# Strassen products of a feed-forward continued in their PSUM banks, with the mixed weights' sums on GpSimd

## The chip, the cores and the metric

The kernel runs on one core of one Trainium2 chip. The metric is the device time of one execution in microseconds (us). Each time is the median of several runs. The profile is of one more execution, taken by the hardware profiler; its times are counted from the start of its span.

The engines are TensorE (PE; its weight loads are PEld), VectorE (DVE), ScalarE (ACT), GpSimd (POOL) and SyncE (SP), which here only issues DMA transfers. Each works through its own instructions in order and waits on semaphores for the others. PSUM is the memory that TensorE writes its products to; it has eight banks here, seven of which the matrix products rotate through.

## The reference

One step of a hybrid decoder layer over 1032 token columns (1024 of a prompt, 8 single tokens), in float32. Cut to what matters here:

```python
h = rms_norm(x, norm_mix_pre)
q, k, v, u, gates = split(h @ w_in)
a = dilated_attention(q, k, v) @ w_attn_out          # three head groups
c = conformer_conv(u) @ w_conv_out
mix = (sigmoid(gate_a) * a + sigmoid(gate_c) * c) @ w_out
x = x + rms_norm(mix, norm_mix_post)
h2 = rms_norm(x, norm_ffn_pre)
gg, uu = split(h2 @ w_ffn_in)                        # 1024 -> 2 x 2816
f = (silu(gg) * uu) @ w_ffn_out                      # 2816 -> 1024
x = x + rms_norm(f, norm_ffn_post)
x = x + sigmoid(rms_norm(x, ple_norm) @ w_ple_gate) * (p @ w_ple_proj)
```

The change lies in `h2 @ w_ffn_in` and the `silu(gg) * uu` behind it.

## The kernel before, in words

Activations stand transposed: 128 channels on the partitions, the 1032 tokens along the free axis. Each float32 operand is split in two parts, hi (ScalarE rounds it to the format fp32r) and lo (the rest, a subtraction), and a product is three matmuls: hi x hi, hi x lo, lo x hi (`mm3`, L278 to L280). In the profile, names that end in h and l are these parts.

The stages, by the span's clock: attention, convolution and the input projections to about 770 us; w_out, the normalisation chains and the first three of the 22 hidden blocks (`hidden_plain`, j = 0 to 2) to 934; the other 19 hidden blocks (`hidden_strassen`, j = 3 to 21) to 1317; the product with w_ffn_out in five groups to 1560 (`ffn_out`, hidden rows loaded back by `load_hidden`); the embedding stage to the end.

A hidden block j is 128 rows of gg and 128 of uu. `hidden_strassen` computes a 2 x 2 block product (gg and uu by the upper and lower half of the input channels, over two quarters of the tokens) with seven products in place of eight. p = 0, 1 are the two pairs of token quarters (258 columns each); the seven products go in the order 1, 2, 6, 5, 7, 3, 4. Each product is four k steps of three matmuls of 128 x 258, in a bank of its own, and when it ends VectorE or ScalarE reads the bank. The running sums are kept in the four quarters of a tile `pk`: x, v, s, w. VectorE makes one addition out of PSUM for each product after the first, and a second one for product 7. In the end x holds silu(gg) * uu of one quarter and v of the other; a DMA stores them to DRAM (`d_h`).

The weights of the seven products come from `prepare(j)`: from the two loaded weight tiles a and b (`raw`, 128 x 1024 each, halves a1, a2, b1, b2) it makes s1 = b1 + b2, s2 = s1 - a1, s3 = a1 - b1, s4 = a2 - s2, and splits a, the four sums and b2 into hi parts (ScalarE) and lo parts (VectorE): wah/wal for the products 1 and 2, wbh/wbl for 6 and 5, wch/wcl for 7 and 3, wd for 4. `prepare(j + 1)` is a generator, of which one step is taken behind each product of block j; in the last block `first_hidden` takes its place and loads the first four hidden pairs of the next stage. `fetch` and `ensure` load weights three tiles ahead (`rawp`, 3 buffers), so that the load of a tile waits until the one three before it was read.

Nothing sets the order by hand in this part: a scheduler orders each engine's instructions by its own estimate, with the limits that the pools give (43 `act` slots, 4 `sc` and 6 `rl` tiles, the PSUM banks). SP's queue is in order as well: a load that waits for its buffer holds all that stands behind it.

Names that matter below: r is the reciprocal root of a normalisation, on GpSimd (`token_rstd`: a power over 128 x 3); TensorE spreads it over the columns (L337, m<-ident,r). hr is a hidden pair loaded from `d_h`, uh and ul its hi and lo parts (ScalarE, VectorE). L120 is the helper that records every instruction but the matmuls.

Of the kernel before, what the change touches and what calls it, by code (L numbers as in the profile page):

```python
# [16 lines left out]
P = 128  # L17
# [41 lines left out]
def decoder_step(ctx: ExitStack, tc: tile.TileContext, ins, outs):  # L59
# [24 lines left out]
    def act(s, dt=F32):  # L84
        return actp.tile([P, SLOT], dt, tag="act", name=nm(s))
# [9 lines left out]
    def bank():  # L95
        gtags.rotate(-1)
        t = gtags[-1]
        return (psg if t == "g" else psa).tile([P, 512], F32, tag=t, name=nm("g"))
# [166 lines left out]
    def finish(key):  # L265

        while any(ch[2] == key for ch in chains):
            tick(5)
# [5 lines left out]

        return c if isinstance(c, tuple) else CH[c]

    def mm3(ps, n, hi_w, lo_w, xh, xl, first, last):
        TE.matmul(ps, hi_w, xh, start=first, stop=False)  # L278
        TE.matmul(ps, hi_w, xl, start=False, stop=False)  # L279
        TE.matmul(ps, lo_w, xh, start=False, stop=last)  # L280

    def gemm_bank(wi, xs, c, nk=KT, mid=None, at=MID):

# [1041 lines left out]
    def prepare(j):  # L1325
# [6 lines left out]

        def split(src, hi, lo):
            A.activation(hi, src, AF.Copy)
            V.tensor_sub(lo, src, hi.bitcast(F32))

        def halves(hi, lo):
            return [(hi[:, i * H:(i + 1) * H], lo[:, i * H:(i + 1) * H]) for i in range(2)]
# [3 lines left out]
        w[1], w[2] = halves(hi, lo)  # L1342
        yield
        s1, s2 = sc("s1"), sc("s2")
        V.tensor_add(s1, b1, b2)
        V.tensor_sub(s2, s1, a1)
        w[6], w[5] = halves(act("wbh", F32R), act("wbl", F32R))
        split(s2, *w[6])
        yield
        split(s1, *w[5])  # L1350
        yield
        s3 = sc("s3")
        V.tensor_sub(s3, a1, b1)
        w[7], w[3] = halves(act("wch", F32R), act("wcl", F32R))
        split(s3, *w[7])
        yield
        s4 = sc("s4")
        V.tensor_sub(s4, a2, s2)
        split(s4, *w[3])
        yield  # L1360
        d = act("wd", F32R)
        w[4] = d[:, :H], d[:, H:2 * H]
        split(b2, *w[4])

    def hidden_strassen(j, nxt):
        for p in range(2):
            finish(2)
            finish(("t", p))
            t0 = 2 * p * QN
            quarter = {1: (0, 0), 2: (4, 0), 3: (4, QN)}  # L1370
            pk = act("pk")
            x, v, s, w = (pk[:, i * QN:(i + 1) * QN] for i in range(4))
            for m in (1, 2, 6, 5, 7, 3, 4):
                ps = bank()[:, :QN]
                wh, wl = prods[j][m]
                for k in range(4):
                    if m in quarter:
                        f, o = quarter[m]
                        xh, xl = (y[:, t0 + o:t0 + o + QN] for y in h2[f + k])
                    else:  # L1380
                        xh, xl = (y[:, k * QN:(k + 1) * QN] for y in tsum[p][{5: 0, 6: 1, 7: 2, 4: 3}[m]])
                    mm3(ps, QN, wh[:, k * P:(k + 1) * P], wl[:, k * P:(k + 1) * P], xh, xl, k == 0, k == 3)
                if m == 1:
                    A.activation(x, ps, AF.Copy)
                elif m == 2:
                    V.tensor_add(s, x, ps)
                    A.activation(s, s, AF.Silu)
                elif m == 6:
                    V.tensor_add(x, x, ps)
                elif m == 5:  # L1390
                    V.tensor_add(v, x, ps)
                elif m == 7:
                    V.tensor_add(w, v, ps)
                    V.tensor_add(x, x, ps)
                elif m == 3:
                    V.tensor_add(v, v, ps)
                    A.activation(v, v, AF.Silu)
                    V.tensor_mul(v, v, w)
                else:
                    V.tensor_add(x, x, ps)  # L1400
                    V.tensor_mul(x, x, s)
                tick(1.3)
                next(nxt, None)
            SY.dma_start(d_h[j, :, t0:t0 + 2 * QN], pk[:, :2 * QN])
        del prods[j]

    for js, qs in [(range(2), range(2)), ((2,), (0,)), (range(2), (2,)), ((2,), (1, 2))]:
# [250 lines left out]
```

## Time and profile before

| | us |
|---|---|
| median of 3 runs | 1694.67 (1694.48 to 1694.79) |
| span of the profiled execution | 1692.8 |
| TensorE busy | 1676.1 |
| VectorE busy | 1195.4 |
| ScalarE busy | 610.5 |
| GpSimd busy | 23.1 |
| Strassen blocks, 934 to 1318: TensorE busy | 384.00 of 384.00 |
| the same stretch: VectorE, ScalarE busy | 256.29, 119.29 |

The page lists the busy time of each engine and follows the chain of work that ended last. A row of a listing in order of time gives the start and the duration in us, the engine, the line, the operation, output<-inputs, shapes and count, and in brackets the engine's idle time before it with what ended it. A row of a grouped listing gives the count, then the busy us of the group, the mean ns of one, and the idle time ahead of it.

### The profile page before, as it was taken

The page shows a single profiled execution, that of the slowest core. Times are in us where ns is not written, and L with a number is a line of the kernel's source. Part 1 is how long each engine was busy: PE and PEld are TensorE (multiplying, and loading weights), DVE is VectorE, ACT ScalarE, POOL GpSimd, SP SyncE. Part 2 cuts the span into 40 slices and gives each one's busy share as a digit, 9 for nine tenths or more (in the row PEclk, how much of TensorE's full clock was granted, in tenths as well). Part 3 has the DMA queues.
Part 4 walks back from the last instruction along what each step waited for, and adds up shares of the span by engine and source line. Part 5 has one row for each costly group of instructions (what it writes and reads, how often), then busy time and mean ns, then how long its engine had stood idle before and what let it go on. Part 6 is the DMA issues. An engine that isn't in the chain of part 4 may idle for free.

```text
span 1692.8 us, 28641 instructions
## 1 busy us (share of the span) xinstructions
PE 1676.1 (99%) x11651; PEld 1649.1 (97%) x11651; DVE 1195.4 (71%) x2084; ACT 610.5 (36%) x1231; POOL 23.1 (1%) x33
## 2 busy tenths in 40 slices
PE   8999999999999999999999999999999999999998
PEld 7999999999999999999999999999999999999998
DVE  7899879858979686553679666666666445548863
ACT  6434445445343344123445323323323311213520
POOL 1000000000000000000000000000000000000000
PEclk9999999999999999999999999999999999999999
DMA  5241121121354264423242222323333533420411
GB/s 191 65 125 66 44 68 45 61 81 53 102 177 159 92 196 128 142 73 121 85 128 78 82 98 89 100 89 113 111 108 125 182 109 114 162 97 13 159 51 47
DMA packets 80889, 174.64 MB, mean 103 GB/s; under 512 B 11154, under 2 KB 49890, under 8 KB 80374
## 3 DMA queue, kind: packets, MB, share of 16 engines
q1 hardware_dynamic: 80566, 172.69, 31.3%
q8 instruction: 91, 1.49, 0.4%
q0 software_dynamic: 192, 0.13, 0.1%
q14 instruction: 40, 0.33, 0.1%
HBM read 136.16 MB, written 50.13 MB: 110 GB/s over the span
## 4 chain that ended last, share of the span: by engine, by line
PE 92%; DVE 4%; issue 1%; DMA 1%; ACT 1%; POOL 0%; SPq 0%; POOLq 0%; DVEq 0%; ACTq 0%
PE g L278 29%; PE g L280 29%; PE g L279 29%; DVE y L120 3%; PE O L675 1%; PE S L630 1%; PE PT L657 1%; DVE wl L120 1%; PE m L337 0%; DMA res<-d_x 0%; PE m L325 0%; DMA strow<-in_state_conv_dram 0%; DVE acc L120 0%; POOL r L120 0%; DMA raw<-in_w_in_dram 0%
## 5 line engine op out<-in xcount | busy, mean ns | idle before, releaser
L278 PE MATMUL g<-hh,wh 128*128 128x384 f32 (+1 forms) x1200 | 393.1, 328 | 7.1 <-ACT wh L120 7.1
L280 PE MATMUL g<-hh,wl 128*128 128x384 f32 (+1 forms) x1200 | 384.3, 320 | 0.2 <-DVE wl L120 0.2
L279 PE MATMUL g<-hl,wh 128*128 128x384 f32 (+1 forms) x1200 | 383.9, 320 | 0.0
L120 DVE SCALAR_TENSOR_TENSOR y<-z,taps,y 128x1023 f32<-128x1023 f32 (+14 forms) x240 | 303.9, 1267 | 36.7 <-ACT y L120 31.1
L278 PEld LDWEIGHTS g<-hh,wh 128*128 128x128 f32 x1200 | 226.4, 189 | 14.4 <-ACT wh L120 7.1
L279 PEld LDWEIGHTS g<-hl,wh 128*128 128x128 f32 x1200 | 226.3, 189 | 0.6 <-DVE hl L120 0.3
L280 PEld LDWEIGHTS g<-hh,wl 128*128 128x128 f32 x1200 | 225.9, 188 | 0.8 <-DVE wl L120 0.8
L280 PE MATMUL g<-uh,wl 128*128 128x344 f32 x528 | 168.7, 320 | 0.0
L279 PE MATMUL g<-ul,wh 128*128 128x344 f32 x528 | 168.6, 320 | 0.0
L278 PE MATMUL g<-uh,wh 128*128 128x344 f32 x528 | 163.2, 321 | 0.6 <-DVE fa L120 0.6
L120 DVE TENSOR_TENSOR wl<-raw,wh 128x1024 fp32r<-128x1024 f32 x106 | 129.0, 1220 | 35.1 <-ACT wh L120 28.6
L120 DVE TENSOR_TENSOR pk<-pk,g 128x258 f32<-128x258 f32 x266 | 105.4, 420 | 55.1 <-PE g L280 39.3
L120 ACT ACTIVATE wh<-raw 128x1024 fp32r<-128x1024 f32 x106 | 110.7, 1051 | 7.1 <-PE g L279 3.8
L278 PE MATMUL g<-mh,wh 128*128 128x344 f32 x336 | 107.4, 323 | 0.0
L280 PE MATMUL g<-mh,wl 128*128 128x344 f32 x336 | 107.1, 320 | 0.0
L279 PE MATMUL g<-ml,wh 128*128 128x344 f32 x336 | 107.0, 320 | 0.0
L120 DVE TENSOR_TENSOR fa<-fa,g 128x344 f32<-128x344 f32 x96 | 47.1, 510 | 77.2 <-PE g L280 76.7
L279 PEld LDWEIGHTS g<-ul,wh 128*128 128x128 f32 x528 | 99.3, 188 | 0.0
L280 PEld LDWEIGHTS g<-uh,wl 128*128 128x128 f32 x528 | 99.2, 188 | 0.0
L278 PEld LDWEIGHTS g<-uh,wh 128*128 128x128 f32 x528 | 98.0, 188 | 0.9 <-DVE fa L120 0.9
L278 PE MATMUL g<-th,wbh 128*128 128x258 f32 x304 | 86.0, 283 | 0.0
L279 PE MATMUL g<-ml,wah 128*128 128x258 f32 x304 | 85.9, 283 | 0.0
(234 smaller groups left out, 3687.1 us busy)
## 6 DMA issues: line engine op xcount, KB each, us to landing
raw<-in_w_in_dram SPq DMA_DIRECT2D x50, 512.0 KB
raw<-in_w_ffn_in_dram SPq DMA_DIRECT2D x44, 512.0 KB
hr<-d_h SPq DMA_DIRECT2D x22, 516.0 KB
raw<-in_w_ffn_out_dram SPq DMA_DIRECT2D x22, 512.0 KB
d_h<-pk SPq DMA_DIRECT2D x38, 258.0 KB
out_kvs_dram<-in_cache_kv_w_dram SPq DMA_DIRECT2D x16, 510.0 KB
d_x<-mo SPq DMA_DIRECT2D x24, 172.0 KB
out_yT_dram<-fa SPq DMA_DIRECT2D x24, 172.0 KB
```

What stands on the lines that cost most here:

```text
L120: ins = fn(*a, **k)
L278: TE.matmul(ps, hi_w, xh, start=first, stop=False)
L279: TE.matmul(ps, hi_w, xl, start=False, stop=False)
L280: TE.matmul(ps, lo_w, xh, start=False, stop=last)
L630: TE.matmul(sp[h][:, o:o + nk], qT[h * 64:(h + 1) * 64, blk * P:(blk + 1) * P], kT[h * 64:(h + 1) * 64, (blk + 1) * P - nk:(blk + 1) * P], ...
L657: TE.transpose(ps[:, o:o + P], e[:, o:o + P], ident)
L675: TE.matmul(ps[h * 64:(h + 1) * 64, i * P:(i + 1) * P], vtok[:, k0:k0 + 64], self.p[half][:, o:o + P], start=kb == kbs[0], stop=kb == kbs[-1])
```

## The change

It has three parts.

- In `hidden_strassen` (now with a class `Quad`) the products share three banks: 1, 6, 7 and 4 one after the other in B1, 2 in B2, 5 and 3 in B3. Only the products 1, 2 and 5 open a bank; the others add to what is there (`more` in `mm3` marks a group of matmuls that goes on). So a bank holds p1, then p1 + p6, and so on, and the sums that the addition trees made are already there. What is needed of a bank before it is added to is read out first: ScalarE copies it after the products 1, 6 and 5 into `rl` tiles (p1, p6, p5). VectorE adds PSUM to such a copy after 2, 7 and 3, and multiplies PSUM by x after 4.
- For j over 3 the two pairs go product by product (1 of pair 0, 1 of pair 1, 2 of pair 0, ...), with one store of `pk` for each pair at the block's end. Block 3 does one pair after the other.
- In `prepare` the four sums and the six lo parts are made by GpSimd: per block nine operations of 128 x 512 and one of 128 x 1024.

```diff
--- before.py
+++ after.py
@@ -274,10 +274,10 @@
 
         return c if isinstance(c, tuple) else CH[c]
 
-    def mm3(ps, n, hi_w, lo_w, xh, xl, first, last):
-        TE.matmul(ps, hi_w, xh, start=first, stop=False)
-        TE.matmul(ps, hi_w, xl, start=False, stop=False)
-        TE.matmul(ps, lo_w, xh, start=False, stop=last)
+    def mm3(ps, n, hi_w, lo_w, xh, xl, first, last, more=False):
+        TE.matmul(ps, hi_w, xh, start=first, stop=False, skip_group_check=more)
+        TE.matmul(ps, hi_w, xl, start=False, stop=False, skip_group_check=more)
+        TE.matmul(ps, lo_w, xh, start=False, stop=last, skip_group_check=more)
 
     def gemm_bank(wi, xs, c, nk=KT, mid=None, at=MID):
 
@@ -1332,7 +1332,7 @@
 
         def split(src, hi, lo):
             A.activation(hi, src, AF.Copy)
-            V.tensor_sub(lo, src, hi.bitcast(F32))
+            G.tensor_sub(lo, src, hi.bitcast(F32))
 
         def halves(hi, lo):
             return [(hi[:, i * H:(i + 1) * H], lo[:, i * H:(i + 1) * H]) for i in range(2)]
@@ -1342,66 +1342,102 @@
         w[1], w[2] = halves(hi, lo)
         yield
         s1, s2 = sc("s1"), sc("s2")
-        V.tensor_add(s1, b1, b2)
-        V.tensor_sub(s2, s1, a1)
+        G.tensor_add(s1, b1, b2)
+        G.tensor_sub(s2, s1, a1)
         w[6], w[5] = halves(act("wbh", F32R), act("wbl", F32R))
         split(s2, *w[6])
         yield
         split(s1, *w[5])
         yield
         s3 = sc("s3")
-        V.tensor_sub(s3, a1, b1)
+        G.tensor_sub(s3, a1, b1)
         w[7], w[3] = halves(act("wch", F32R), act("wcl", F32R))
         split(s3, *w[7])
         yield
         s4 = sc("s4")
-        V.tensor_sub(s4, a2, s2)
+        G.tensor_sub(s4, a2, s2)
         split(s4, *w[3])
         yield
         d = act("wd", F32R)
         w[4] = d[:, :H], d[:, H:2 * H]
         split(b2, *w[4])
 
+    ORDER = (1, 2, 6, 5, 7, 3, 4)
+    B1, B2, B3 = range(3)
+    BANK = {1: B1, 6: B1, 7: B1, 4: B1, 2: B2, 5: B3, 3: B3}
+    OPENS = (1, 2, 5)
+
+    class Quad:
+
+
+        def __init__(self, j, p):
+            self.j, self.p, self.t0 = j, p, 2 * p * QN
+            self.banks, self.part = {}, {}
+            self.pk = act("pk")
+
+        def piece(self, i):
+            return self.pk[:, i * QN:(i + 1) * QN]
+
+        def operand(self, m, k):
+            quarter = {1: (0, 0), 2: (4, 0), 3: (4, QN)}
+            if m in quarter:
+                f, o = quarter[m]
+                return tuple(y[:, self.t0 + o:self.t0 + o + QN] for y in h2[f + k])
+            return tuple(y[:, k * QN:(k + 1) * QN] for y in tsum[self.p][{5: 0, 6: 1, 7: 2, 4: 3}[m]])
+
+        def product(self, m):
+            if m in OPENS:
+                self.banks[BANK[m]] = bank()[:, :QN]
+            ps = self.banks[BANK[m]]
+            wh, wl = prods[self.j][m]
+            for k in range(4):
+                xh, xl = self.operand(m, k)
+                mm3(ps, QN, wh[:, k * P:(k + 1) * P], wl[:, k * P:(k + 1) * P], xh, xl,
+                    k == 0 and m in OPENS, k == 3, m not in OPENS)
+
+        def after(self, m):
+            x, v = self.piece(0), self.piece(1)
+            ps = self.banks[BANK[m]]
+
+            def keep(name):
+                t = rl(name)[:, :QN]
+                A.activation(t, ps, AF.Copy)
+                self.part[m] = t
+
+            if m == 1:
+                keep("p1")
+            elif m == 2:
+                V.tensor_add(x, self.part[1], ps)
+                A.activation(x, x, AF.Silu)
+            elif m == 6:
+                keep("p6")
+            elif m == 5:
+                keep("p5")
+            elif m == 7:
+                w = self.part[5]
+                V.tensor_add(w, w, ps)
+            elif m == 3:
+                V.tensor_add(v, self.part[6], ps)
+                A.activation(v, v, AF.Silu)
+                V.tensor_mul(v, v, self.part[5])
+            else:
+                V.tensor_mul(x, ps, x)
+
     def hidden_strassen(j, nxt):
-        for p in range(2):
-            finish(2)
-            finish(("t", p))
-            t0 = 2 * p * QN
-            quarter = {1: (0, 0), 2: (4, 0), 3: (4, QN)}
-            pk = act("pk")
-            x, v, s, w = (pk[:, i * QN:(i + 1) * QN] for i in range(4))
-            for m in (1, 2, 6, 5, 7, 3, 4):
-                ps = bank()[:, :QN]
-                wh, wl = prods[j][m]
-                for k in range(4):
-                    if m in quarter:
-                        f, o = quarter[m]
-                        xh, xl = (y[:, t0 + o:t0 + o + QN] for y in h2[f + k])
-                    else:
-                        xh, xl = (y[:, k * QN:(k + 1) * QN] for y in tsum[p][{5: 0, 6: 1, 7: 2, 4: 3}[m]])
-                    mm3(ps, QN, wh[:, k * P:(k + 1) * P], wl[:, k * P:(k + 1) * P], xh, xl, k == 0, k == 3)
-                if m == 1:
-                    A.activation(x, ps, AF.Copy)
-                elif m == 2:
-                    V.tensor_add(s, x, ps)
-                    A.activation(s, s, AF.Silu)
-                elif m == 6:
-                    V.tensor_add(x, x, ps)
-                elif m == 5:
-                    V.tensor_add(v, x, ps)
-                elif m == 7:
-                    V.tensor_add(w, v, ps)
-                    V.tensor_add(x, x, ps)
-                elif m == 3:
-                    V.tensor_add(v, v, ps)
-                    A.activation(v, v, AF.Silu)
-                    V.tensor_mul(v, v, w)
-                else:
-                    V.tensor_add(x, x, ps)
-                    V.tensor_mul(x, x, s)
-                tick(1.3)
-                next(nxt, None)
-            SY.dma_start(d_h[j, :, t0:t0 + 2 * QN], pk[:, :2 * QN])
+        for group in ((0,), (1,)) if j == CLASSIC else ((0, 1),):
+            quads = []
+            for p in group:
+                finish(2)
+                finish(("t", p))
+                quads.append(Quad(j, p))
+            for m in ORDER:
+                for q in quads:
+                    q.product(m)
+                    q.after(m)
+                    tick(1.3)
+                    next(nxt, None)
+            for q in quads:
+                SY.dma_start(d_h[j, :, q.t0:q.t0 + 2 * QN], q.pk[:, :2 * QN])
         del prods[j]
 
     for js, qs in [(range(2), range(2)), ((2,), (0,)), (range(2), (2,)), ((2,), (1, 2))]:
```

How the instructions stand then. GpSimd's queue has 36 rows before and 226 with the change. Around the last normalisation ahead of block 3 it read, before (r1 is a power for one third of the tokens):

```order
L120 TENSOR_TENSOR r1_1129_8420<-r0_1128_8418,mhalf_101 128x3
L120 TENSOR_TENSOR r1_1161_8644<-r0_1160_8642,mhalf_101 128x3
L120 TENSOR_TENSOR r1_1171_8763<-r0_1170_8761,mhalf_101 128x3
L120 TENSOR_TENSOR r1_1210_8996<-r0_1209_8994,mhalf_101 128x3
L120 TENSOR_TENSOR r1_2073_15861<-r0_2072_15859,mhalf_101 128x3
L120 TENSOR_TENSOR r1_2109_16103<-r0_2108_16101,mhalf_101 128x3
```

and it reads with the change:

```order
L120 TENSOR_TENSOR r1_1161_8644<-r0_1160_8642,mhalf_101 128x3
L120 TENSOR_TENSOR r1_1171_8763<-r0_1170_8761,mhalf_101 128x3
L120 TENSOR_TENSOR s1_1269_9429<-raw_1218_9023 128x512
L120 TENSOR_TENSOR s2_1270_9430<-s1_1269_9429,raw_1215_9017 128x512
L120 TENSOR_TENSOR r1_1210_8996<-r0_1209_8994,mhalf_101 128x3
L120 TENSOR_TENSOR s3_1273_9439<-raw_1215_9017,raw_1218_9023 128x512
L120 TENSOR_TENSOR s4_1276_9445<-raw_1215_9017,s2_1270_9430 128x512
L120 TENSOR_TENSOR wal_1268_9426<-raw_1215_9017,wah_1267_9425 128x1024
L120 TENSOR_TENSOR wbl_1272_9434<-s2_1270_9430,wbh_1271_9433 128x512
L120 TENSOR_TENSOR wbl_1272_9434<-s1_1269_9429,wbh_1271_9433 128x512
```

The power r1_1210 now stands behind the sums s1 and s2 of block 3, which wait for the weight tiles raw_1218 and raw_1215.

SyncE's queue at the end of the last block and the start of the next stage, before (pk_1800 and pk_1823 are the two pairs of block 21, hr_1808 to hr_1833 the first four hidden pairs):

```order
L120 DMA hr_1808_13872<-d_h_84 128x1032
L120 DMA raw_1812_13893<-in_w_ffn_out_dram 128x1024
L120 DMA d_h_84<-pk_1800_13808 128x516
L120 DMA hr_1816_13915<-d_h_84 128x1032
L120 DMA raw_1820_13936<-in_w_ffn_out_dram 128x1024
L120 DMA hr_1825_13958<-d_h_84 128x1032
L120 DMA raw_1829_13979<-in_w_ffn_out_dram 128x1024
L120 DMA hr_1833_13999<-d_h_84 128x1032
L120 DMA d_h_84<-pk_1823_13943 128x516
L120 DMA out_kvs2_dram<-in_cache_kv_w2048_dram 16x8160
L120 DMA raw_1846_14112<-in_w_ffn_out_dram 128x1024
L120 DMA hr_1849_14118<-d_h_84 128x1032
```

and with the change (pk_1764 and pk_1765 are the pairs of block 21, hr_1775, hr_1783, hr_1793 and hr_1799 the first four hidden pairs):

```order
L120 DMA hr_1775_13768<-d_h_84 128x1032
L120 DMA raw_1779_13788<-in_w_ffn_out_dram 128x1024
L120 DMA hr_1783_13808<-d_h_84 128x1032
L120 DMA raw_1788_13829<-in_w_ffn_out_dram 128x1024
L120 DMA d_h_84<-pk_1764_13700 128x516
L120 DMA d_h_84<-pk_1765_13701 128x516
L120 DMA out_kvs2_dram<-in_cache_kv_w2048_dram 16x8160
L120 DMA hr_1793_13850<-d_h_84 128x1032
L120 DMA raw_1796_13869<-in_w_ffn_out_dram 128x1024
L120 DMA hr_1799_13888<-d_h_84 128x1032
```

The third and the fourth hidden pair's loads stood ahead of the last store of pk; now both stores and a copy of a cache stand ahead of them, and ahead of those the weight load raw_1788.

VectorE at the same place, with the change (p5 holds w; the last two rows of pk are the products by silu out of PSUM):

```order
L120 TENSOR_TENSOR pk_1764_13700<-p6_1778_13786,g_1786_13814 128x258
L120 TENSOR_TENSOR pk_1764_13700<-pk_1764_13700,p5_1787_13827 128x258
L120 TENSOR_TENSOR pk_1765_13701<-p6_1782_13806,g_1791_13835 128x258
L120 TENSOR_TENSOR ul_1777_13770<-hr_1775_13768,uh_1776_13769 128x1032
L120 TENSOR_TENSOR pk_1765_13701<-pk_1765_13701,p5_1792_13848 128x258
L120 TENSOR_TENSOR wl_1781_13791<-raw_1742_13483,wh_1780_13790 128x1024
L120 TENSOR_TENSOR pk_1764_13700<-g_1766_13702,pk_1764_13700 128x258
L120 TENSOR_TENSOR pk_1765_13701<-g_1768_13717,pk_1765_13701 128x258
L120 TENSOR_TENSOR ul_1785_13810<-hr_1783_13808,uh_1784_13809 128x1032
L120 TENSOR_TENSOR wl_1790_13832<-raw_1771_13747,wh_1789_13831 128x1024
```

and before, for the last pair alone:

```order
L120 TENSOR_TENSOR pk_1823_13943<-pk_1823_13943,g_1828_13964 128x258
L120 TENSOR_TENSOR pk_1823_13943<-pk_1823_13943,g_1832_13985 128x258
L120 TENSOR_TENSOR pk_1823_13943<-pk_1823_13943,g_1836_14005 128x258
L120 TENSOR_TENSOR pk_1823_13943<-pk_1823_13943,g_1837_14019 128x258 x2
L120 TENSOR_TENSOR pk_1823_13943<-pk_1823_13943,g_1838_14034 128x258
L120 TENSOR_TENSOR pk_1823_13943<-pk_1823_13943,g_1839_14050 128x258
L120 TENSOR_TENSOR pk_1823_13943<-pk_1823_13943 128x258
L120 TENSOR_TENSOR ul_1827_13960<-hr_1825_13958,uh_1826_13959 128x1032
L120 TENSOR_TENSOR wl_1831_13982<-raw_1812_13893,wh_1830_13981 128x1024
L120 TENSOR_TENSOR pk_1823_13943<-pk_1823_13943 128x258
```

The subtraction wl_1781, which frees the raw buffer that the load raw_1788 waits for, stands behind ul_1777 and the second pair's product by p5; before, the first loads' ul and wl stood ahead of the last pair's additions.

## The prediction

> **What bounds the kernel now.** I read the page first (busy shares, slices, the chain), then stretches of it by stage, then the matmuls of the changed stage one by one, and last the queues at its two ends. The page's first two sections and its chain:
>
> ```profile
> span 1692.8 us, 28641 instructions
> ...
> PE 1676.1 (99%) x11651; PEld 1649.1 (97%) x11651; DVE 1195.4 (71%) x2084; ACT 610.5 (36%) x1231; POOL 23.1 (1%) x33
> ...
> PEclk9999999999999999999999999999999999999999
> ...
> PE 92%; DVE 4%; issue 1%; DMA 1%; ACT 1%; POOL 0%; SPq 0%; POOLq 0%; DVEq 0%; ACTq 0%
> ```
>
> TensorE is busy for 99% of the span at a full clock, and 92% of the chain is its own. The span is 1.87 us under the median of the runs, 1694.67. I add differences to the span and carry them over to the median unchanged. By stage (each engine: busy us and its instructions):
>
> ```profile
> 770.00:934.00 164.00, 164.00 (x1056) 163.48 (x1056) 116.28 (x250) 76.35 (x157) 5.13 (x6) 1.00 0.33 104
> 934.00:1318.00 384.00, 384.00 (x3198) 384.00 (x3198) 256.29 (x523) 119.29 (x227) 0.00 (x0) 1.00 0.32 104
> 1318.00:1560.00 242.00, 240.56 (x1529) 239.47 (x1528) 127.79 (x217) 55.90 (x78) 2.55 (x3) 1.00 0.33 113
> ```
>
> The first three numbers after the stretch are TensorE, its weight loads and VectorE in order, then ScalarE and GpSimd. The second row is the changed stage, the 19 Strassen blocks: TensorE 384.00 of 384.00, VectorE 256.29 (67%), GpSimd nothing. Its first and last matmul, and the first of the next stage:
>
> ```profile
> 934.14 0.28 PE L278 MATMUL g<-mh,wah 128*128 128x258 f32 x1
> ...
> 1317.30 0.28 PE L280 MATMUL g<-th,wd 128*128 128x258 f32 x1
> 1317.42 0.32 PE L278 MATMUL g<-uh,wh 128*128 128x344 f32 x1
> ```
>
> 19 blocks of 14 products of 12 matmuls are 3192. From 934.14 to 1317.42 that is 383.28 us, or 0.1201 us a matmul, 1.441 a product, 20.17 a block. The neighbouring starts in these listings lie 0.11 to 0.13 apart. So there is no gap in the stage for the change to close: work taken off VectorE there is worth nothing by itself. The time can change only where TensorE comes to wait, or stops waiting, and I looked for that.
>
> **The change part by part.** First, the matmuls: as many, of the same sizes, with the partial sums left in a bank in place of being added up later. TensorE's work: 0.
>
> Second, VectorE's and ScalarE's share of a quad. These are the costs of a block's work on VectorE in the stage (count over the stage, then busy us, mean ns):
>
> ```profile
> L120 DVE TENSOR_TENSOR pk<-pk,g 128x258 f32<-128x258 f32 x264 | 104.7, 420 | 55.1 <-PE g L280 39.3 <-ACT pk L120 10.3
> L120 DVE TENSOR_TENSOR pk<-pk 128x258 f32<-128x258 f32 x74 | 30.1, 426 | 10.8 <-ACT pk L120 9.0
> L120 DVE TENSOR_TENSOR wbl<-s,wbh 128x512 fp32r<-128x512 f32 x36 | 23.3, 688 | 33.0 <-PE g L279 33.0
> L120 DVE TENSOR_TENSOR wal<-raw,wah 128x1024 fp32r<-128x1024 f32 x18 | 22.0, 1224 | 11.9 <-ACT wah L120 11.9
> ```
>
> A quad had seven additions out of PSUM and two products on VectorE, 9 x 0.42 = 3.8 us; it now has three additions and two products, 2.1. Per block 3.4 us leave VectorE, and the weights' nine halves and one whole, 9 x 0.69 + 1.22 = 7.4, leave too: 10.8 of some 13.5. ScalarE gains two copies a quad, 4 x 0.39 = 1.5 us a block. All of it lies beside 20.17 us of matmuls: 0.
>
> What is new is a deadline. Products 1, 6, 7 and 4 share a bank, and 5 and 3 another, so the matmuls of 6 wait for the copy of p1, those of 7 for that of p6, those of 3 for that of p5, those of 4 for w's addition. In blocks 4 to 21 both pairs run product by product, and three products, 4.3 us, lie between a product's end and the next in its bank; a read costs 0.22 until it starts and 0.4. The longest thing ahead on ScalarE is two splits of 0.6. Cost 0. In block 3 the pairs run one after the other, and there only one product, 1.44 us, lies between. Its tightest place is p5 of the second pair, about 950, where today stands on ScalarE:
>
> ```profile
> 947.34 1.16 ACT L120 ACTIVATE wch<-s 128x512 fp32r<-128x512 f32 x2 [3.44 <-PE g L280]
> 950.14 0.63 ACT L120 ACTIVATE wd<-raw 128x512 fp32r<-128x512 f32 x1 [1.65 <-issue]
> 950.68 0.37 ACT L120 ACTIVATE pk<-g 128x258 f32<-128x258 f32 x1
> ```
>
> With the wd split ahead of it the copy ends by 951.1. Product 5 of the second pair is the eleventh of the block (product 3 the thirteenth: it starts at 934.14 + 12 x 1.441 = 951.4). Margin 0.3 us: 0, with up to 1 us if it is missed.
>
> Third, GpSimd. It had no such operation in 1692.8 us; the nearest rows are these:
>
> ```profile
> L120 POOL TENSOR_TENSOR r<-r,mhalf 128x3 f32<-128x3 f32 x18 | 16.3, 907 | 1165.8 <-DVE r L120 1165.8
> ...
> L120 POOL MEMSET bias<- 128x512 f32 x1 | 0.5, 532 | 2.0 <-PE g L280 2.0
> ...
> L120 POOL MEMSET sbias<- 128x12 f32 x1 | 0.1, 104 | 0.0
> ```
>
> Call X the time of one sum of 128x512. Below, VectorE's 0.69. A fill of 512 costs 0.10 and 0.43 for the elements; two operands in and one out at that rate each make 0.10 + 3 x 0.43 = 1.39, which I take as the value and as nearest in kind (same engine, same size). A block then costs 9 x 1.39 + 2.7 = 15.2 us, under 20.17. GpSimd becomes the bound from 11 X = 20.17, X = 1.83. In the steady state weights are made about a block ahead of use, so any X under that costs 0. In block 3 they are not: behind the sums come its low parts, and the wcl half of the product 7 that is the fifth (939.9) is ready about 933, wd's about 938 to 939 against 942.8. Cost 0.
>
> Fourth, GpSimd's queue ahead of block 3. There the sums s1 and s2 now stand ahead of the power r1 that the last normalisation waits for. Today:
>
> ```profile
> 892.89 0.33 SPq L120 DMA_DIRECT2D raw<-in_w_ffn_in_dram  x1
> ...
> 897.17 0.16 DVE L120 TENSOR_SCALAR r<-cs 128x3 f32<-128x3 f32 x1
> ...
> 897.50 0.87 POOL L120 TENSOR_TENSOR r<-r,mhalf 128x3 f32<-128x3 f32 x1 [18.38 <-DVE r L120]
> ...
> 899.52 0.49 PE L337 MATMUL m<-ident,r 128*128 128x128 f32 x3
> ...
> 899.80 0.68 DVE L120 TENSOR_TENSOR s<-raw,raw 128x512 f32<-128x512 f32 x1
> ...
> 900.40 1.53 DVE L120 SCALAR_TENSOR_TENSOR mo<-mo,vecs,m 128x344 f32<-128x344 f32 x3
> ```
>
> The input of s1 and s2 is the load issued at 892.89. A load of that kind takes about 3.3 us here (an estimate: ScalarE's first use of such a load, below, comes 3.7 after the issue), so they run from 896.2 to 896.2 + 2 x 1.39 = 899.0, and r1 ends at 899.9. TensorE's transposes want it at 899.52. So +0.4. Bounds: with X = 0.69 it ends at 898.5, 0; with X = 1.83 it ends at 900.7, 1.2; a first operation that runs as long again as the power itself adds 0.9, so up to 1.9. The normalisation's scaling itself may begin earlier, since s1 to s4 left VectorE's queue (the row at 899.80 ended just ahead of it).
>
> The Trainium skill ("SBUF — State Buffer", section "Who interferes with whom") says that a VectorE instruction with two SBUF inputs and a GpSimd instruction that reads SBUF shut each other out for a whole instruction. The one place here where both run, the power from 897.50 to 898.37, does not show it: VectorE's product of two SBUF tiles at 897.58 took 0.42, as elsewhere. By that rule the term here would be larger; it is the third rival below.
>
> Fifth, the end of the last block. SP's queue is one line, and each load of a hidden pair (hr) stands in it behind what is written before it. Today, with ScalarE's first use of what it brought:
>
> ```profile
> 1308.87 0.38 SPq L120 DMA_DIRECT2D hr<-d_h  x1
> ...
> 1311.15 0.38 SPq L120 DMA_DIRECT2D hr<-d_h  x1
> ...
> 1316.52 0.38 SPq L120 DMA_DIRECT2D hr<-d_h  x1
> 1322.16 0.32 SPq L120 DMA_DIRECT2D d_h<-pk  x1
> 1322.53 0.52 SPq L120 DMA_DIRECT2D out_kvs_dram<-in_cache_kv_w_dram  x1
> ...
> 1323.77 0.38 SPq L120 DMA_DIRECT2D hr<-d_h  x1
> ```
>
> ```profile
> 1312.60 1.07 ACT L120 ACTIVATE uh<-hr 128x1032 fp32r<-128x1032 f32 x1 [3.53 <-DMA hr<-d_h]
> ...
> 1321.72 1.07 ACT L120 ACTIVATE uh<-hr 128x1032 fp32r<-128x1032 f32 x1 [1.66 <-DMA hr<-d_h]
> ...
> 1329.73 1.07 ACT L120 ACTIVATE uh<-hr 128x1032 fp32r<-128x1032 f32 x1 [6.00 <-DMA hr<-d_h]
> ```
>
> Today the third and fourth load (1311.15, 1316.52) go ahead of the last store of pk. In the new order the third stands behind a weight load, both last stores and a 510 KB copy. The weight load needs the raw buffer that wl_1781 frees. That stands on VectorE behind ul_1777 and the second pair's v x p5. In the clock of before: product 3 of the second pair, the twelfth of 14, ends at 1297.26 + 12 x 1.441 = 1314.6; read and silu to 1315.7, ul to 1316.4, v x p5 to 1316.8, wl to 1318.0. Then x of both pairs (0.42 each, to 1318.8), the stores' and the copy's issues (0.37, 0.6), and the third load leaves at 1319.8. Landing to ScalarE took 3.73, 5.20 and 5.96 us in the rows above (1308.87, 1316.52, 1323.77). The last two, with a copy or a store beside them, are nearest; their middle, 5.6, gives 1325.4. Then uh 1.07 and ul 1.23: 1327.7. TensorE, which starts the next stage at 1317.42 and does 42 and 46 matmuls of 0.158 us before the first that need uh and ul of this load, wants ul at 1324.7. So a wait of 3.0 us; by the 3.73 row 1.1, by the 5.96 row 3.4, and 4.5 if its issue drags on by the 1.11 us that one such took. The fourth load then comes just in time. What covers this today is the early place in the queue; it is gone.
>
> Sixth, a gain. One wait of the next stage lies in a place where a bank is read just ahead of its next use:
>
> ```profile
> 1339.96 0.32 PE L280 MATMUL g<-uh,wl 128*128 128x344 f32 x1
> 1340.89 0.42 PE L278 MATMUL g<-uh,wh 128*128 128x344 f32 x1 [0.61 <-DVE fa L120]
> ```
>
> 0.93 between starts against 0.16: 0.77 us. In the new order such reads stand at least eleven matmuls ahead. So -0.8 (0 if it reappears elsewhere).
>
> Sum: +3.0 + 0.4 - 0.8 = +2.6: span 1695.4, time 1697.3. No difference that a measurement of this kernel can tell from none is under about 0.2%, 3.4 us: it lies between 1691.3 and 1698.1, so this is "the same", near its slow edge.
>
> **The rivals.**
> 1. The hidden load comes in time. If the copy's queue place costs little and it lands 2.6 us after issue, no wait is left: +0.4 - 0.8, time 1694.3. Against it: no hr row shows less than 3.73.
> 2. Slower, by that same load alone: the wait reaches 3.8 or more (landing over 6.4 us, since 510 KB of copy and 512 KB of weights are in flight with it): +3.4 and up. At 5 us of wait 1699.3. For it: today's slowest, 5.96, was the one with copy and weight load both ahead, as here. From 3.8 us on it decides.
> 3. The shut-out at the head: s1, s2 and r1 each wait for one VectorE operation of 0.42 with two SBUF inputs: +1.3, time 1698.6, slower. Against it stands the row at 897.58.
> 4. TensorE waits inside the blocks, because a read of p1, p6 or w comes late each time: from 0.2 us a block it is 18 x 0.2 = 3.6, with the sum above 1700.9. Against it: 4.3 us of room.
> 5. GpSimd the bound, X over 1.83: at X = 2.2 a block takes 24.2 in place of 20.17, 18 x 4.0 = +73, time about 1770.
> 6. Faster: fewer VectorE reads of PSUM let the matmuls run closer. 3.4 us over 3192 of them is 1.1 ns each, 0.9%. Against it: the spacing is 0.12 whether VectorE reads or not (at 934 to 937, with no product to read, 0.12 as well).
>
> **How the numbers follow.** Forecast 0.41, rival 1 0.13, 2 0.20, 3 0.08, 4 0.08, 5 0.06, 6 0.04. Same is the forecast and 1, 0.54 (some of the forecast's own spread, 1695 to 1698.1, ends there); slower 2 to 5, 0.42; faster 0.04. The range leaves out 5, 6 and the far parts of 2 and 4: 1693.5 to 1703. The forecast's own range is 1695.0 to 1698.1.
>
> **What would show it.** Right: TensorE 384 of 384 in the blocks; a wait of about 3 us on the third uh or ul some 7 us into the next stage; none like that of 1340.89; a wait of some 0.4 on POOL r near 899.5; GpSimd busy for 19 x 11 X with X about 1.4. Wrong: gaps between matmuls at product starts in the blocks (rival 4 or 5), an hr load issued ahead of the last stores, or a sum of GpSimd that is far longer beside VectorE than alone.

## The result and the profile after

The changed kernel takes 1709.33 us (1707.94 to 1714.38, four runs) against 1694.58 before: 1.0091 times as long, with an interval of 1.0078 to 1.0103. That is 14.8 us slower, and outside the range of the prediction, which was 1697.3 (1693.5 to 1703). The profiled execution took 1709.87, with a span of 1708.1, 15.3 us over that of before.

The page of the changed kernel, the same parts as before:

```profile
PE 1681.4 (98%) x11651; PEld 1653.5 (97%) x11651; DVE 1036.4 (61%) x1742; ACT 634.0 (37%) x1307; POOL 288.9 (17%) x223
...
PE 88%; DVE 6%; issue 2%; DMA 1%; ACT 1%; POOL 1%; SPq 0%; POOLq 0%; DVEq 0%; ACTq 0%
```

VectorE is 159 us lighter, GpSimd 266 us heavier, and TensorE's share of the chain fell from 92 to 88%. TensorE's matmuls are as many as before, yet its busy time grew by 5.3 us: some of them ran slower. What it waited for, in us in total, times and longest (left out is one wait of 7.1 us on ACT wh at the start, which both kernels have):

```profile
PE g L278 <- ACT p L120: 7.0, 3, 4.3
PE g L278 <- ACT uh L120: 3.3, 1, 3.3
PE m L337 <- POOL r L120: 3.2, 4, 1.0
PE g L278 <- ACT mh L120: 0.8, 1, 0.8
```

ACT p are ScalarE's copies of p1, p6 or p5, which the change added; uh is the third hidden pair; r and mh belong to the last normalisation. These are four places. They follow in order of time, each with TensorE's row and that of the matmul before it: the difference of the two starts, less the usual 0.12 or 0.16, is the wait.

**The last normalisation, 2.2 us.**

```profile
898.57 0.32 PE L280 MATMUL g<-mh,wl 128*128 128x344 f32 x1
899.90 0.54 PE L337 MATMUL m<-ident,r 128*128 128x128 f32 x3 [1.00 <-POOL r L120]
...
901.38 0.32 PE L280 MATMUL g<-mh,wl 128*128 128x344 f32 x1
902.53 0.89 PE L278 MATMUL g<-mh,wh 128*128 128x344 f32 x4 [0.82 <-ACT mh L120]
```

**Block 3, 2.3 and 0.8 us.** Product 6 of the first pair waits for the copy of p1, and product 7 for that of p6. VectorE, ScalarE and TensorE there:

```profile
937.09 2.93 DVE L120 TENSOR_TENSOR t<-mo,t 128x258 f32<-128x258 f32 x2
939.94 4.02 DVE L120 TENSOR_TENSOR tl<-t,th 128x258 fp32r<-128x258 f32 x2
```

```profile
938.64 0.42 ACT L120 ACTIVATE th<-t 128x258 fp32r<-128x258 f32 x1 [1.93 <-DVE t L120]
940.05 0.42 ACT L120 ACTIVATE th<-t 128x258 fp32r<-128x258 f32 x1 [0.99 <-DVE t L120]
940.38 0.37 ACT L120 ACTIVATE p<-g 128x258 f32<-128x258 f32 x1
```

```profile
938.38 0.28 PE L280 MATMUL g<-mh,wal 128*128 128x258 f32 x1
940.80 0.58 PE L278 MATMUL g<-th,wbh 128*128 128x258 f32 x1 [2.13 <-ACT p L120]
941.18 0.42 PE L279 MATMUL g<-tl,wbh 128*128 128x258 f32 x1
941.39 0.42 PE L280 MATMUL g<-th,wbl 128*128 128x258 f32 x1
...
944.17 0.28 PE L278 MATMUL g<-th,wbh 128*128 128x258 f32 x1
...
946.01 0.39 PE L278 MATMUL g<-th,wch 128*128 128x258 f32 x1 [0.61 <-ACT p L120]
```

Product 1 was done by 937.2, and its copy ran at 940.38: it stood on ScalarE behind two hi parts of token sums (th), these waited for VectorE's t, and two t took 2.93 us. One took 0.42 in the kernel before:

```profile
932.35 0.42 DVE L120 TENSOR_TENSOR t<-mo,t 128x258 f32<-128x258 f32 x1
```

TensorE's rows hold a second cost: behind the first wait the matmuls start 0.21 apart in place of 0.12, for 3.4 us, until 944.17. In this time the granted TensorE clock was half; it is the third number from the end of the row for this stretch:

```profile
940.71:944.12 3.41, 3.32 (x15) 3.33 (x16) 3.41 (x3) 0.55 (x2) 2.97 (x2) 0.50 0.48 151
```

The trace records two more such stretches, from 991.91 and 1340.07, each 3.41 us long. The row of the granted clock on the page has tenths of 40 slices and shows 9 throughout.

**Block 5, 4.4 us.** Again a product 6, now the second pair's, and its copy of p1. The chain goes back through three queues (the second column is the duration, SPq is SyncE's queue of DMA issues):

```profile
984.23 1.28 POOL L120 TENSOR_TENSOR wd<-raw,wd 128x512 fp32r<-128x512 f32 x1
```

```profile
985.53 0.33 SPq L120 DMA_DIRECT2D raw<-in_w_ffn_in_dram  x1
985.92 0.90 SPq L120 DMA_DIRECT2D d_h<-pk  x2
```

```profile
982.37 0.39 ACT L120 ACTIVATE p<-g 128x258 f32<-128x258 f32 x1 [2.60 <-PE g L280]
990.80 1.15 ACT L120 ACTIVATE wbh<-s 128x512 fp32r<-128x512 f32 x2 [8.04 <-DMA d_h<-pk]
991.86 0.37 ACT L120 ACTIVATE p<-g 128x258 f32<-128x258 f32 x1
```

```profile
987.75 0.28 PE L280 MATMUL g<-th,wbl 128*128 128x258 f32 x1
992.28 0.58 PE L278 MATMUL g<-th,wbh 128*128 128x258 f32 x1 [4.26 <-ACT p L120]
```

GpSimd's wd ends at 985.5 and frees a raw buffer; only then does SyncE issue the weight load, and behind it the stores of pk, whose x was ready at 981.3 (VectorE's last row of block 4: 980.86, 0.43). The next wbh takes a tile that one of the stores must have read. It stands on ScalarE ahead of the second pair's copy of p1, which therefore came at 991.86.

This is no cost of every block. Block 5 starts at 980.66, so wd ended 4.8 us into the block. From block 6 on it ends some 0.75 us ahead of the block's start (1005.97 against 1006.73), the queue is the same, and TensorE does not wait. GpSimd was late from block 3 on: the wd of the blocks 3 and 4 ended 5.6 and 4.7 us into them.

**The next stage, 3.4 us,** where the prediction had put a wait of 3.0 on the third hidden pair:

```profile
1330.12 0.33 SPq L120 DMA_DIRECT2D raw<-in_w_ffn_out_dram  x1
1330.55 0.87 SPq L120 DMA_DIRECT2D d_h<-pk  x2
1331.47 0.52 SPq L120 DMA_DIRECT2D out_kvs_dram<-in_cache_kv_w_dram  x1
1332.08 0.98 SPq L120 DMA_DIRECT2D hr<-d_h  x1
```

```profile
1336.25 0.32 PE L280 MATMUL g<-uh,wl 128*128 128x344 f32 x1
1339.86 1.35 PE L278 MATMUL g<-uh,wh 128*128 128x344 f32 x4 [3.28 <-ACT uh L120]
```

The four matmuls from 1339.86 take 1.26 us from the first start to the next row's (1341.12), about twice their 0.16 each: slow again.

The account: 2.2 ahead of block 3; 2.3 + 0.8 + 4.4 waiting in the blocks and 3.1 lost behind those waits, nearly all in slow matmuls (1.6 behind the first, 1.4 behind the third, 0.1 behind the second); 3.4 and 1.8 in the next stage, less the 0.8 of the wait at 1340.9 that is gone. That is 17.2, and the span grew by 15.3. The other stages, which the change leaves alone, were 1.7 shorter in all (0.8 up to 770 us, 0.9 at the end); the product with w_ffn_out grew by 0.5 less than its terms, the blocks by 0.2 more.

### The profile page after: what moved, and what is told of

Read it like the earlier page. It is cut to its first block, busy times and chain, and to the rows that moved or that the text cites. A ratio compares the mean times of both kernels' runs of the same rounds, so it can differ in the third digit from the quotient of the medians.

```text
span 1708.1 us, 28632 instructions
## 1 busy us (share of the span) xinstructions
PE 1681.4 (98%) x11651; PEld 1653.5 (97%) x11651; DVE 1036.4 (61%) x1742; ACT 634.0 (37%) x1307; POOL 288.9 (17%) x223
## 4 chain that ended last, share of the span: by engine, by line
PE 88%; DVE 6%; issue 2%; DMA 1%; ACT 1%; POOL 1%; SPq 0%; POOLq 0%; DVEq 0%; ACTq 0%
PE g L278 28%; PE g L280 28%; PE g L279 28%; DVE y L120 3%; PE O L675 1%; PE S L630 1%; PE PT L657 1%; DVE tl L120 1%; DVE t L120 1%; DMA d_h<-pk 1%; DVE wl L120 1%; POOL s L120 0%; DMA hr<-d_h 0%; PE m L337 0%; PE m L325 0%
## 5 line engine op out<-in xcount | busy, mean ns | idle before, releaser
L120 POOL TENSOR_TENSOR r<-r,mhalf 128x3 f32<-128x3 f32 x18 | 16.4, 910 | 752.8 <-DVE r L120 752.7
L120 DVE TENSOR_TENSOR pk<-p,g 128x258 f32<-128x258 f32 x76 | 31.0, 421 | 126.5 <-PE g L280 97.8
L120 DVE TENSOR_TENSOR p<-p,g 128x258 f32<-128x258 f32 x38 | 16.1, 425 | 138.1 <-ACT p L120 77.2
```

The lines of the kernel that those rows point to most:

```text
L120: ins = fn(*a, **k)
```

## The experiments

Theory A is the account above. Theory B holds that the continued banks cost the time by themselves; theory C that GpSimd's weights are what comes late. Each kernel was timed against the kernel before on the same chip.

**Weights back on VectorE** (e1): in `prepare`, every `G.tensor_sub`/`G.tensor_add` is `V.` again.

> The changed kernel with all sums and low parts of the mixed weights back on VectorE; the products still continue in their banks, in the same pair order. Theory A (the time went to four places: GpSimd and VectorE shutting each other out ahead of block 3, the stores of pk held in SP's queue behind loads that wait for GpSimd, the late third hidden load at the end, and a slower TensorE clock behind each long wait): the first two go with GpSimd, the last load stays, so about 1694.6 + 4 = 1698.5 us, with the stage of the blocks at 383 to 385 us and one wait of about 3.4 us some 7 us into the next stage. Theory B (the continued banks cost it, since each product must wait for a copy of the one before): waits in the blocks stay, 1704 us or more.

1698.91 against 1694.36 (1.0029, interval 1.0019 to 1.0039): theory A's number. The blocks are full, and only the last place is left, a wait of 3.5 us on ACT uh. The row of the stage, TensorE first:

```profile
934.00:1318.00 384.00, 384.00 (x3197) 384.00 (x3196) 199.75 (x373) 141.58 (x302) 0.00 (x0) 1.00 0.31 99
```

So the continued banks with their copies cost no wait in the blocks: their span is 383.5 us, 383.3 before. Theory B is out.

**GpSimd alone** (e2): `hidden_strassen` as before, `prepare` on GpSimd.

> The kernel before with the sums and low parts of the mixed weights on GpSimd, each product in a bank of its own as before. Theory A: the late power of the last normalisation stays (+2.2 us by the changed kernel's trace), VectorE operations ahead of block 3 still stretch to 1 to 3 us, but no product waits for a copy of the one before it in its bank, and the last stores stand as before: about 1697 us, between 1696 and 1699. Theory B: no waits in the blocks at all and none at the head, 1694.6 us. Theory C (GpSimd's late weights are what TensorE waits for): waits on GpSimd's weights, 1704 us or more.

1694.90 (1.0003, 0.9993 to 1.0013): no difference that can be told. The profile has both waits of the normalisation (2.0 us together) and none in the blocks; on the time their 2 us are not to be seen beside runs that differ by 2.2 us, and theory A's 1697 was too high. VectorE's rows from 950 to 1318 in this kernel (count | busy us, mean ns):

```profile
L120 DVE TENSOR_TENSOR pk<-pk,g 128x258 f32<-128x258 f32 x253 | 101.5, 421 | 180.6 <-ACT pk L120 98.8 <-PE g L280 67.8 <-POOL wcl L120 9.9
L120 DVE TENSOR_TENSOR pk<-pk 128x258 f32<-128x258 f32 x72 | 51.9, 730 | 30.5 <-ACT pk L120 28.6
```

With an operand in PSUM an operation takes 421 ns, as before (420); with both in SBUF 730, where it took 426. GpSimd's work does reach VectorE, and with a bank for each product TensorE does not mind. Theory C is out as well. The waits in the blocks need the two parts together; the one in the next stage comes without GpSimd too (e1).

**Only the weights of blocks 3 and 4 on VectorE** (e3): `E = V if j <= CLASSIC + 1 else G`, and `E.` in `prepare`.

> The changed kernel with the weights of blocks 3 and 4 alone made by VectorE, those of blocks 5 to 21 by GpSimd. Theory A: nothing of GpSimd runs beside the token sums ahead of block 3, so the late power (2.2 us), the wait of 2.3 us in block 3 with its slow matmuls (about 4 us) and the late start of GpSimd go: the loads are freed in time, the wait of 4.4 us in block 5 goes as well, about 1698.5 us, the last hidden load's wait being left. If the stores of pk stay behind the loads by themselves, waits in block 5 or later stay: 1703 to 1705 us. Theory B: 1705 us or more.

1701.61 (1.0046, 1.0030 to 1.0061). The normalisation's waits, those for copies of p1 and p6 and that in block 5 are gone; 17 blocks still take their weights from GpSimd, and the stores of pk still stand behind loads that wait for its wd. One wait of 1.1 us on w's addition in block 3 is new, the last hidden load's 3.3 us is left. The time is 3.1 us over the expected one. In the profiled run, of 1703.5, a wait of 2.0 us at 1628 with slow matmuls behind it came on top, on a power that took 1.80 in place of 0.85; why is open, and whether the other runs had it too.

**The last block's pairs one after the other** (e4): `if j in (CLASSIC, NH - 1)`.

> The changed kernel with the two pairs of the last block (21) one after the other, as in block 3, so that the first four hidden loads stand ahead of the last store of pk in SP's queue again. Theory A: the wait of 3.4 us and the slow matmuls behind it in the next stage go (about 4.7 us), the rest stays: 1704 to 1705 us. If the hidden load was late for another reason (memory traffic), the wait stays, 1709 us.

A miss: 1712.85 (1.0104, 1.0086 to 1.0122). In the profiled run the wait in the next stage was still 2.9 us, and the blocks took 395.9 us in place of 394.1. The third load did stand ahead of the last store, but left only at 1333.15, 0.6 us after the next stage began (its first matmul: 1332.6). A weight load stood ahead of it, that one waited for VectorE's wl, and wl for ScalarE's wh:

```profile
1328.49 0.39 ACT L120 ACTIVATE p<-g 128x258 f32<-128x258 f32 x1 [1.01 <-PE g L280]
1328.77 1.06 ACT L120 ACTIVATE uh<-hr 128x1032 fp32r<-128x1032 f32 x1
1329.73 1.05 ACT L120 ACTIVATE wh<-raw 128x1024 fp32r<-128x1024 f32 x1
```

The first uh and wh now stood behind the late copies of the last pair. So the place behind the stores is not all of the mechanism; the weight load ahead of the hidden load holds it as well.

**The first hidden loads from GpSimd's queue** (e5): `(G if j < HID[0] else SY).dma_start(r, d_h[j])`.

> The changed kernel with the first four hidden loads (hr) issued from GpSimd's queue, which is idle by then, in place of SyncE's. Theory A: the third load no longer stands behind the weight load that waits for VectorE's wl, nor behind the last stores and the copy; the wait of 3.4 us in the next stage and the slow matmuls behind it go, the next stage takes 253 us in place of 257.8, the time is 1709.3 - 4.7 = 1704.6 us. If it is late for memory traffic or for want of a free buffer, the wait stays: 1709 us.

1706.37 (1.0071, 1.0056 to 1.0086). The wait in the next stage is gone, and with it its slow matmuls: from the stage's first matmul to the first of the embedding stage 253.0 us, where the changed kernel has 257.8 and the kernel before 253.9. The time fell by 3.0, not 4.7; the profiled run shows why in part: it was 0.9 us later up to 770, and its blocks took 1.2 us more. In block 3, whose program is the same, the wait for p1 (2.3) had no slow matmuls behind it there, while the wait for p6 was 2.25 in place of 0.8 and had them. The third load left at 1318.99, 12 us ahead of the stage.

**The stores from ScalarE's queue** (e6): `A.dma_start(d_h[...], q.pk[...])` in place of `SY.`

> The changed kernel with the blocks' stores of pk issued from ScalarE's queue, right behind its last work on the block, in place of SyncE's, where each stands behind a weight load that waits for GpSimd's wd. Theory A: the wait of 4.4 us in block 5 and its slow matmuls (about 5.8 us) go, the waits ahead of and in block 3 and at the end stay: about 1703.5 us. Rival (GpSimd itself is late, so its weights are what is missing in block 5): the wait stays or moves to a wbl or wcl: 1708 to 1710 us.

1700.24 (1.0035, 1.0023 to 1.0046). Block 5's wait is gone; ScalarE's rows there:

```profile
976.85 1.92 ACTq L120 DMA_DIRECT2D d_h<-pk  x2
979.32 0.39 ACT L120 ACTIVATE p<-g 128x258 f32<-128x258 f32 x1 [2.61 <-PE g L280]
979.60 1.15 ACT L120 ACTIVATE wbh<-s 128x512 fp32r<-128x512 f32 x2
980.74 0.39 ACT L120 ACTIVATE p<-g 128x258 f32<-128x258 f32 x1
```

The store leaves when the block's x is done, and wbh no longer waits for it. It went further than expected: the next stage's wait is gone too (253.1 us), since the hidden loads no longer stand behind the stores. In the profiled run, of 1696.22, block 3's two waits were 1.2 us each and no slow matmuls followed. The other five runs lie at 1700.0 to 1701.7, with a mean granted clock of 0.998 to 0.999 in place of 1.000: the trace is of the fastest run, and the others may have had waits and slow matmuls that it does not show.

**The sums of block 3 on VectorE** (e7): s1 to s4 for j = CLASSIC alone on `V`.

> The changed kernel with the four sums s1 to s4 of block 3 alone on VectorE; its low parts and all of the later blocks stay on GpSimd. Theory A: the power r is no longer behind the sums, so the two waits at 899.9 and 902.5 (2.2 us together) go; VectorE's token sums still stretch to 1.5 to 3 us beside GpSimd's low parts from 920 on, so the wait in block 3 (2.3 us) and what follows it stay: about 1707 us. If the shutting out is not what delays block 3 (but the late scaling of the last third), that wait goes too: about 1700 to 1703 us.

1709.95 (1.0095, 1.0080 to 1.0110). The normalisation's two waits are gone, block 3's are not (2.6 and 2.3 us): they do not need the late scaling, and VectorE's operations on token sums are stretched here as well:

```profile
933.68 0.50 DVE L120 TENSOR_TENSOR sl<-g,sl 128x344 f32<-128x344 f32 x1
934.10 2.54 DVE L120 TENSOR_TENSOR tl<-t,th 128x258 fp32r<-128x258 f32 x2
936.57 2.92 DVE L120 TENSOR_TENSOR t<-mo,t 128x258 f32<-128x258 f32 x2
```

The 2.2 us did not show in the time: up to 770 us the profiled run was 1.4 us later than the changed kernel's, and its blocks took 0.4 and the next stage 0.5 us more.

**The continued banks alone, loads from GpSimd's queue** (e8): e1 and e5 together.

> The continued banks and the pair order alone, with all weights on VectorE and the first four hidden loads from GpSimd's queue. Theory A: nothing of the four places is left, and the wait of 0.77 us at 1340.9 of the kernel before is gone too: 1694.4 - 0.8 = 1693.6 us, the stage of the blocks 383.3 us. If the continued banks cost anything by themselves it is over 1694.4 us.

1693.74 against 1694.48 (0.9995, 0.9986 to 1.0005). No wait over 0.2 us is left between 934 and 1548; the one of 0.77 is gone too. The 0.7 us by which it is faster cannot be told from none.

**Both mended, GpSimd kept** (e9): e3 and e6 together.

> The changed kernel with two mends: the weights of blocks 3 and 4 on VectorE, those of blocks 5 to 21 on GpSimd; and the stores of pk from ScalarE's queue. Theory A: no wait is left of the four places but the one of 0.9 us on w's addition in block 3 that such a block 3 showed before; the blocks take 384 us, the next stage 253 us, the time is 1694 to 1695.5 us, the same as the kernel before. Rival (GpSimd beside the blocks costs TensorE something all along): 1697 us or more.

1694.75 against 1694.43 (1.0000, 0.9990 to 1.0009). GpSimd makes the weights of 17 blocks and TensorE has one gap of 1.1 us in block 3:

```profile
934.00:1318.00 384.00, 383.05 (x3188) 382.84 (x3187) 98.32 (x203) 142.60 (x302) 237.07 (x170) 1.00 0.31 102
```

VectorE has 98 us to do in the stage in place of 256, and nothing is won: the time is that of the kernel before.

**GpSimd busy for nothing** (e10): in the kernel before, behind block 3's first split,

```diff
+        if j == CLASSIC:
+            scrap = rl("scrap")
+            for _ in range(16):
+                G.tensor_add(scrap, hi[:, :CW].bitcast(F32), hi[:, H:H + CW].bitcast(F32))
```

> The kernel before with 16 additions of 128x384 on GpSimd, from two halves of wah into a scrap tile that nothing reads, just when the weights of block 3 are split (from about 923 us on). All other engines keep their order. Theory A: while they run (some 16 us), VectorE operations with both inputs in SBUF (t, tl, wbl, wcl: 0.42 and 0.69 us) take 1 to 1.5 us, those with one input from PSUM (sl) keep 0.52; the weights of block 3 come late, TensorE waits 1 to 8 us: 1696 to 1705 us. If GpSimd and VectorE do not shut each other out: every duration as before, 1694.5 us.

1695.11 (1.0004, 0.9995 to 1.0014): a miss in the time, where 1696 to 1705 were expected; the durations came out as theory A has them. The additions ran from 930.96 on. VectorE and, last, GpSimd:

```profile
932.37 0.42 DVE L120 TENSOR_TENSOR t<-mo,t 128x258 f32<-128x258 f32 x1
...
934.48 1.23 DVE L120 TENSOR_TENSOR t<-mo,t 128x258 f32<-128x258 f32 x1
935.63 1.50 DVE L120 TENSOR_TENSOR s<-raw 128x512 f32<-128x512 f32 x1
...
939.64 0.50 DVE L120 TENSOR_TENSOR sl<-g,sl 128x344 f32<-128x344 f32 x1
```

```profile
930.96 14.44 POOL L120 TENSOR_TENSOR scrap<-wah 128x384 f32<-128x384 f32 x9 [31.29 <-DVE wbl L120]
```

The operations with SBUF operands alone go from 0.42 to 1.23 and from 0.69 to 1.50, though nothing reads what GpSimd makes; sl, with an operand in PSUM, keeps 0.50. Up to 933.3 it was GpSimd that waited: its first addition took 3.31 us, and VectorE's operations kept 0.42 and 0.69. Started eight us later than expected, the additions met few of block 3's weights: TensorE had one wait of 1.1 us at 958.

## Why the prediction was wrong, point by point

- **The bound, right.** TensorE had no gap to close, and work taken off VectorE won nothing: e9 has 98 us of it in place of 256 in the stage, at the same time.
- **"Block 3 ... margin 0.3 us: 0", wrong.** I looked for the tightest copy on ScalarE with the durations of before. The copies that failed were those of p1 and p6 of the first pair, behind the hi parts of the last token sums, whose low and sum operations GpSimd stretched. The failure is in the step on the shutting out: the one overlap in the trace of before was a GpSimd power over three columns, and I took its silence for evidence against the rule. With 384 to 1024 columns in GpSimd's operations the rule of the Trainium skill ("SBUF — State Buffer", "Who interferes with whom") holds in e2, e7 and e10.
- **"In the steady state ... any X under that costs 0", right from block 6 on, but block 5 paid 4.4 us.** GpSimd was not the bound: X came out at 1.30, where 1.39 was taken, a block's work at 9 x 1.30 + 2.42 = 14.1 of 20.17 us (mean ns behind the busy time):

```profile
L120 POOL TENSOR_TENSOR wcl<-s,wch 128x512 fp32r<-128x512 f32 x38 | 48.8, 1304 | 49.6 <-ACT wch L120 48.8 <-ACT th L120 0.8
...
L120 POOL TENSOR_TENSOR wal<-raw,wah 128x1024 fp32r<-128x1024 f32 x19 | 46.0, 2421 | 28.1 <-ACT wah L120 20.6 <-PE g L280 7.5
```

  But each store of pk stands in SyncE's queue behind a weight load that waits for GpSimd's wd, and in the blocks 3 to 5 wd was late. I followed that queue at the program's end only, and took GpSimd's start as timely. With either one taken away the wait went: e6 took the store out of the queue, e3 took the blocks 3 and 4 from GpSimd and left the queue as it was.
- **The normalisation, mis-sized.** +0.4 was forecast for r; it was 1.2 on r and 1.0 on mh behind it, which I had left out: its scaling stood on VectorE behind stretched low parts (the third rival's mechanism, priced at 1.3). Of the 1.2, some 0.6 is the weight load: the sums began 3.9 us after its issue, where 3.3 was taken. VectorE's own row of r, which the power needs as well, took 1.25 in place of 0.16 and ended with s2 at 898.8, so s1 and s2 are not alone in the delay.
- **The last block, right in place, kind and size:** 3.0 forecast, 3.4 measured. The load left 2.4 us into the stage, as forecast; ScalarE used it 6.7 us later, where 5.6 was taken. e4 to e6 show the two things ahead of the load. What came on top, 1.8 us, is the next point.
- **No term for slow matmuls.** I costed each wait at its own length. Behind three of the waits (2.3, 4.4 and 3.4 us) the granted clock was 0.50 for 3.41 us; of the account above that is 5 us, and without it the sum is some 12. Not all of it is added time: in e4, with the same block 3, no slow matmuls followed the wait for p1, and the wait for p6 was 2.2 us in place of 0.8. So behind the first wait they mostly took the place of waiting.
- **The wait of 1340.9, right:** it is gone in the changed kernel, worth 0.8.
- **The rivals.** The fourth (TensorE waits inside the blocks, from late reads of p1 or w) is what happened, with 0.08; its price was spread over 18 blocks, where in fact two blocks paid 7.5 us. The range ended 6 us too low, since it took the rivals one at a time.

The runs of the changed kernel spread over 6.4 us, those of before over 0.5. Their mean granted clocks are 0.998 (1707.94 and 1708.79 us), 0.997 (1709.87) and 0.996 (1714.38). One stretch of 3.41 us at half clock lowers the mean by 0.001, so these are some two, two, three and four stretches (an estimate from the profiled run's three, good to about one stretch: runs of the kernel before show 0.999 to 1.000). At up to 1.7 us each they may be about half of the spread; the rest is open.

## What to carry to other kernels

A value that used to have a buffer of its own and now has to be read before the next product may start turns every queue ahead of that read into a part of the critical path: follow each of them, the DMA queue too, at both ends and behind a late start, which can cost time blocks later. Work moved to GpSimd takes VectorE's time as well wherever VectorE reads only SBUF; in these runs only operations with an operand in PSUM kept their time beside it. Before moving work off an engine, ask whether the bound waits for that engine at all; here it didn't, and the best of the mended versions equals the kernel before.

## What the runs showed of the hardware

- In e10 VectorE and GpSimd, both on SBUF operands, take turns: 0.42 became 1.23 and 0.69 became 1.50 us on VectorE beside additions of 128x384; with an operand in PSUM 0.50 stayed 0.50, and in e2 0.42 stayed 0.42. Who waits can change: GpSimd's first addition of 128x384 took 3.31 us while VectorE lost nothing, the next eight 1.07 to 1.88, the last seven 1.01 to 1.23.
- GpSimd's addition of 128x512 takes 1.30 us, of 128x1024 2.42, against 0.69 and 1.22 on VectorE.
- The granted TensorE clock fell to 0.50 for 3.41 us at a time (once, in e7, for 6.83). In such a stretch matmuls of 258 columns start 0.214 apart in place of 0.120, and those of 344 columns 0.287 in place of 0.158. Where a trace has several stretches, their starts lie whole multiples of 3.413 us apart (in the changed kernel 51.20 and 348.16 us, 15 and 102 times; in e4 14 and 101 times).
- Cut into steps of that length, from the first full clock to 1685 us, the twelve traces show when it happens (idle times by the modelled ends of the matmuls): all twelve steps at full clock in which TensorE was idle for 1.98 us or more were followed by a stretch at half clock, none with 1.75 or less was; between them 1.82 (e3) was, 1.81 and 1.87 (e7) were not. So the place of a wait counts with its length: of seven waits of 2.2 to 2.6 us in block 3 (changed kernel, e4, e5, e7), three were followed by slow matmuls and four were not, and none of 1.3 us or less was. The Trainium skill ("TensorE: Matmul & The Clock Gate", Part 1) tells of a halved clock behind idle windows of about 3.4 us. The half clock and the 3.41 us agree, but here a window with 2.04 us of idle time (up to 940.71 in the changed kernel) was enough.
